# The opening of a convolution layer laid out anew: shifts as row products, the condition spread by TensorE, weight halves on GpSimd

## Chip, cores and metric

The kernel runs on one core of a Trainium2 chip. The metric is device time in microseconds. The kernel before takes 1960.24 us (median of three runs, 1960.0 to 1963.34).

## What is computed

One layer of a streaming encoder in fp32: 2048 tokens, width 1024, a short gated convolution, then a SwiGLU network. Both sub-layers are normalized before and after, and modulated by shift, scale and gate vectors that come from a condition vector c.

```python
def modulate(h, shift, scale):
    return h * (1.0 + scale[:, None, :]) + shift[:, None, :]

def short_conv_mixer(h, w_in, w_conv, w_out):
    gate_b, gate_c, v = jnp.split(h @ w_in, 3, axis=-1)
    u = gate_c * v
    conv = ...                       # causal, 3 taps, one filter for each channel
    return (gate_b * conv) @ w_out

c_act = jax.nn.silu(c)
mod = c_act @ ada_w[i] + ada_b[i]    # (1024) @ (1024 x 6144)
sh_m, sc_m, g_m, sh_f, sc_f, g_f = jnp.split(mod, 6, axis=-1)
h = modulate(rms_norm(x, norm_gains[i, 0]), sh_m, sc_m)
h = short_conv_mixer(h, ...)
x = x + g_m * rms_norm(h, norm_gains[i, 1])
h = modulate(rms_norm(x, norm_gains[i, 2]), sh_f, sc_f)
h = swiglu(h, ffn_w_gate_up[i], ffn_w_down[i])
return x + g_f * rms_norm(h, norm_gains[i, 3])
```

## The kernel before

**Products.** Tokens are handled in two passes (u = 0, 1) of 1024, each in two halves of 512. The phases follow one another: in0, out0, in1, out1, gu0, down0, gu1, down1 (input projection, output projection, gate and up, down). Each matrix product is split into 2 x 2 blocks and done with seven products instead of eight, P1 to P7. A product takes a sum of weight blocks and a feature: A11, A12, A22 (blocks of the normalized input) or sums of them, S1 to S4. In the first phase the four blocks of the input are called a (token half 0, channel half 0), b (0, 1), c (1, 0) and d (1, 1); e = a - c is the source of S3, d - e of S2, c + d of S1, b - S2 of S4.

Each operand is written as a high half, rounded to the fast matmul type (fp32r), and a low half, the rest. A product of one 128-row step k is three matmuls: high weight by high feature, low by high, high by low. High halves are copies by ScalarE (`high`, `upper`), low halves are subtractions by VectorE (`low`, `lower`, L458 to L465 for the weights). P5 of the first three groups is the exception: it multiplies whole fp32 words.

**Slots.** A slot is one product of one column group, four steps of three matmuls. In in0 the order is P1 of five groups (slots 0 to 4), P2 of five (5 to 9), then P7, P6, P5, P3 and P4 of the first three (10 to 24), and after that seven slots for each further group. The weights of a slot are prepared in stages, each some slots ahead of its use: `blocks` (load, SP's queue, 9 slots), `sums` (T3 and the P6 sum among them, 7), `high` (5), `low` (4). `advance(stage, slot)` takes a stage up to a slot. Work outside the slots is put off with `later`, `run` and `schedule`, all counted in slots. `sums_later("out", ...)` loads the blocks of the output projection, has GpSimd form the four sums of each group, and stores them to DRAM; it starts at slot 24 with two slots between steps. Every instruction is recorded through one helper, so each carries line L78, and each engine and each DMA queue runs its instructions in the order in which the program issues them.

**The opening** is `start()`, written out by hand (L1107 to L1387) up to slot 12. It does the following.

- SP loads the token rows of half 0 (xr), then for each quarter q of the channels the scale matrix (`load_scale`, laid out with one output on each partition) and the shift matrix (`load_shift`, laid out for a matmul), in turn with the blocks a to d and the weights. The rows of token half 1 are loaded before the last scale quarter.
- c comes on all 128 partitions by a DMA of ScalarE's queue (`c_half`, L144 to L146); ScalarE applies silu.
- `squares` (ScalarE), `factor` (VectorE, and GpSimd for the power -1/2), `diagonal` (VectorE) and `spread` (TensorE, copied out by ScalarE) give 1/rms along the free axis as `rb`.
- `scales` are row products on VectorE: one fused multiply and sum of 128 x 512 for each half row, 16 in all. `shifts` are eight fp32 matmuls for each quarter on TensorE (tile pms), with the row copied out by ScalarE and turned by two transposes (`turned`). `fold` puts both into mA (1 + scale, times the gain) and mB (shift).
- `mult` multiplies a feature by rb on VectorE, `shift` is a pass of ScalarE (times mA, plus mB) in place, `upper` and `lower` make the halves, `products` issues matmuls of chosen slots, `follow` takes the sums out of PSUM.
- `warm(n)` issues n fp32 matmuls of ones (tile wb), eight before the first factor and two before the first product.

Of the kernel before, what the change touches and what calls it, by code (L numbers as in the profile page):

```python
# [15 lines left out]
P = 128  # L16
# [15 lines left out]
EARLY = 5  # L32

# [16 lines left out]
def hybrid_conv_layer(  # L50
# [94 lines left out]
    for h in range(2):  # L145
        A.dma_start(c_half[h], c_row[:, h * CH : (h + 1) * CH].to_broadcast((P, CH)))  # L146
# [19 lines left out]
    def columns(row, r, n=4):  # L166

        A.copy(r[0:1, : n * P], row[0:1, : n * P])
        for c in range(n):
            PE.transpose(row[:, c : c + 1], r[0:1, c * P : (c + 1) * P], ident[0:1, 0:1])  # L170

    def mods_later(ms, pace):

        s2 = {(m, h): sb.tile([P, KD], F32, tag="ms", bufs=4, name=f"ms{m}_{h}") for m in ms for h in range(2)}
        for h in range(2):
# [6 lines left out]
            def load(i, half=half, todo=todo, tiles=tiles):  # L182
                if i < len(todo):
                    m, n = todo[i]
                    tiles[i] = raw(f"ada{m}_{half.start}_{n}")
                    SP.dma_start(tiles[i], ada[m - 1, n][:, half])
# [135 lines left out]
    class Blocks:  # L322
# [98 lines left out]
    class Weight:  # L421
# [685 lines left out]
    def start():  # L1107
        ph = phases[0]
        rb, mods, rows, xr = {}, {}, {}, {}
        f = Features(ph, from_xt(0), rb, 0)  # L1110
        s2 = [sb.tile([P, KD], F32, tag="ms", bufs=4, name=f"ms1_{h}") for h in range(2)]
        two = lambda ap: ap.rearrange("p (a b) -> p a b", a=2)
        pair_of = lambda t, i: t[:, 2 * i : 2 * i + 2, :]

# [6 lines left out]
        def load_scale(q):  # L1121

            t = mods[1, q] = big(f"ada1_{q}")
            for i in range(2):
                SP.dma_start(pair_of(t, i), two(ada[0, 2 * q + i]))

        def load_shift(q):

            t = mods[0, q] = big(f"ada0_{q}")
            for i in range(2):  # L1130
                SP.dma_start(pair_of(t, i), two(ada1[2 * q + i]))
# [10 lines left out]
        def factor(tok, meanwhile=lambda: None):  # L1142
# [4 lines left out]
            meanwhile()  # L1147
            return diagonal(at_once(steps), f"r{tok}")

        def shifts(q):  # L1150
            t = mods[0, q].rearrange("p a b -> p (a b)").rearrange("p (k n) -> p k n", k=KD)
            rows[q] = bank(f"pms{q}")
            for k in range(KD):
                PE.matmul(rows[q][0:1, :256], col(cact, k), t[:, k, :], start=k == 0, stop=k == KD - 1)

        def turned(q):
            columns(rows[q], mods[0, q][:, 0, :], 2)

        def scales(q, i):
# [4 lines left out]
        def fold(q):  # L1164
            n = slice(2 * q, 2 * q + 2)
            t = small(2, f"mf{q}")
            V.tensor_tensor(t, s2[0][:, n], s2[1][:, n], ALU.add)
            V.tensor_tensor(t, t, vt[:, VB + KD + n.start : VB + KD + n.stop], ALU.add)
            V.scalar_tensor_tensor(mA[0][:, n], t, 1.0, vt[:, VG + n.start : VG + n.stop], ALU.add, ALU.mult)
            V.tensor_tensor(mB[0][:, n], rows[q][:, :2], vt[:, VB + n.start : VB + n.stop], ALU.add)  # L1170

        def mult(key, k4):
            t = f.t[key][:, k4, :]
            V.tensor_tensor(t, t, rb[f.place[key][0]], ALU.mult)

        def shift(key, k4):
            t, k = f.t[key][:, k4, :], f.place[key][1] * 4 + k4
            A.activation(t, t, AF.Identity, bias=col(mB[0], k), scale=col(mA[0], k))

        def upper(op, k4):  # L1180
            if (op, 0) not in ph.A:
                ph.A[op, 0] = big(f"{ph.name}{op}h", F32R), big(f"{ph.name}{op}l", F32R)
            A.copy(ph.A[op, 0][0][:, k4, :], f.t[f.SOURCE[op]][:, k4, :])

        def lower(op, k4):
            hi, lo = ph.A[op, 0]
            V.tensor_tensor(lo[:, k4, :], f.t[f.SOURCE[op]][:, k4, :], hi[:, k4, :].bitcast(F32), ALU.subtract)
# [15 lines left out]
        load_scale(0)  # L1203
        load_shift(0)
        f.load("a")
        advance("blocks", 2)
        load_scale(1)
        load_shift(1)
        advance("blocks", 4)
        f.load("b")  # L1210
        load_scale(2)
        load_shift(2)
        advance("blocks", 7)
        load_shift(3)
        load_rows(1)
        load_scale(3)
# [5 lines left out]

        def split(key, op, ks):
            for k in ks:
                shift(key, k)
                upper(op, k)
                lower(op, k)
# [10 lines left out]
        warm(8)  # L1238


        squares(0, range(4))
# [12 lines left out]
        fold(0)  # L1254
        mult("a", 3)
        advance("low", 0)
        for k in range(2):
            shift("a", k)
            upper("A11", k)
            lower("A11", k)  # L1260
            advance("high", 1 + k)
            advance("low", 1 + k)
        products(0, range(2))
        scales(1, 0)
        scales(1, 1)
        shifts(1)
        advance("high", 4)
        advance("low", 4)
        products(3, range(2), range(1))
        turned(1)  # L1270
        fold(1)
        products(4, range(2), range(1))
        split("a", "A11", range(2, 4))
        products(0, range(2, 4))
        for k in range(4):
            mult("b", k)
        shifts(2)
        scales(2, 0)
        scales(2, 1)
        products(3, range(2, 4), range(1))  # L1280
        squares(1, range(2))
        turned(2)
        advance("high", 7)
        products(4, range(2, 4), range(1))
        advance("low", 7)
        squares(1, range(2, 4))
        fold(2)
        shifts(3)
        v = small(4, "v1")
        V.tensor_scalar(v, sq[1], EPS, None, ALU.add)  # L1290
        steps = root(v, "r1")
        next(steps)
        shift("b", 0)
        upper("A12", 0)
        scales(3, 0)
        lower("A12", 0)
        shift("b", 1)
        upper("A12", 1)
        scales(3, 1)
        dg = at_once(steps)  # L1300
        lower("A12", 1)
        turned(3)
        fold(3)
        dg = diagonal(dg, "r1")
        products(5, range(2), range(1))
        rb[1] = spread(dg, "r1")
        products(6, range(2), range(1))
        advance("sums", 12)
        shift("b", 2)
        upper("A12", 2)  # L1310
        mult("c", 0)
        lower("A12", 2)
        mult("c", 1)
        shift("b", 3)
        upper("A12", 3)
        lower("A12", 3)
        follow(0, range(3))
        mult("c", 2)
        mult("c", 3)
        products(5, range(2, 4), range(2))  # L1320
        follow(3, range(2))
        advance("high", 9)
        follow(5, range(1))
        advance("low", 8)
        follow(6, range(1))
        products(7, range(4), range(1))
        for k in range(4):
            shift("c", k)
        advance("low", 9)
        products(8, range(4), range(1))  # L1330
        follow(7, range(1))
        products(9, range(4), range(1))

# [3 lines left out]
        def e(k):  # L1337
            V.tensor_tensor(f.t["e"][:, k, :], f.t["a"][:, k, :], f.t["c"][:, k, :], ALU.subtract)
# [3 lines left out]
        advance("high", 10)  # L1342
        e(1)
        follow(8, range(1))
        advance("low", 10)
        lower("S3", 0)
        advance("high", 11)
        advance("low", 11)
        follow(9, range(1))
        lower("S3", 1)  # L1350
        e(2)
        advance("high", 12)
        e(3)
        advance("low", 12)
# [6 lines left out]

        for k in range(4):
            mult("d", k)
            shift("d", k)
        advance("sums", 15)
        advance("high", 15)
        for k in range(4):
            V.tensor_tensor(f.t["a"][:, k, :], f.t["d"][:, k, :], f.t["e"][:, k, :], ALU.subtract)
            upper("S2", k)
            if k:  # L1370
                advance("low", 12 + k)
# [6 lines left out]
        for k in range(4):  # L1378
            V.tensor_tensor(f.t["c"][:, k, :], f.t["c"][:, k, :], f.t["d"][:, k, :], ALU.add)
# [3 lines left out]
        f.s4()  # L1383
        for i, step in ((15, partial(f.high, "S4")), (16, partial(f.low, "S4")),
                        (17, partial(f.high, "A22")), (18, partial(f.low, "A22")),
# [30 lines left out]
    schedule(24, lambda: run(sums_later("out", range(4), 2)))  # L1416
# [98 lines left out]
```

## Time and profile before

| | |
|---|---|
| median of the runs | 1960.24 us (1960.0, 1960.24, 1963.34) |
| the profiled execution | 1961.33 us, span 1959.5 us |
| instructions | 24903 |
| TensorE (PE) busy | 1934.8 us, 8454 matmuls |
| VectorE (DVE) busy | 1446.5 us, 2069 |
| ScalarE (ACT) busy | 899.6 us, 1419 |
| GpSimd (POOL) busy | 343.8 us, 226 |
| moved by DMA | 462.14 MB, mean 236 GB/s |

Times in the profile count from the start of the span. A row of the timeline gives the start in us, the duration in us, engine, line, operation, output<-inputs with buffer numbers left out, sizes and a count where like instructions are merged, and in square brackets the idle time of the engine before it with what ended it. Weight tiles are named by phase and group with digits partly dropped: in4P<-in4b is a low half of a weight of group 4, in0b<-in0P an addition from PSUM. An engine's instructions that follow at once overlap a little, so that the distance from start to start is shorter than the duration.

### The profile page before, as it was taken

How to read it: one execution, taken by the hardware profiler on the slowest of the kernel's cores; microseconds unless marked ns; L12 is line 12 of the kernel's file. 1: busy time of each engine (PE TensorE's matmuls, PEld its weight loads, DVE VectorE, ACT ScalarE, POOL GpSimd, SP SyncE). 2: the span in 40 equal slices, each digit the busy share in tenths (PEclk: the TensorE clock that was granted, in tenths of full speed). 3: DMA queues.
4: the chain of work that ended last, by engine and by line, in shares of the span. 5: the costliest groups of instructions: out<-in, count | busy, mean ns of one | idle time of the engine just before them, and what ended most of it. 6: DMA issues, size and time to landing. Idle time of an engine off the chain costs nothing.

```text
span 1959.5 us, 24903 instructions
## 1 busy us (share of the span) xinstructions
PE 1934.8 (99%) x8454; PEld 1570.0 (80%) x8454; DVE 1446.5 (74%) x2069; ACT 899.6 (46%) x1419; POOL 343.8 (18%) x226
## 2 busy tenths in 40 slices
PE   8899999999999999999999999999999999999998
PEld 4678887878878888888888888888888888888886
DVE  4898898977998776997776755587776655665466
ACT  4543457634446743543333454473333333444452
POOL 0012112211221301243341410120100100111011
PEclk9999999999999999999999999999999999999999
DMA  9369979769996764777665977588654332386534
GB/s 390 138 227 373 339 253 349 268 225 371 323 324 216 279 232 149 238 241 244 213 214 183 313 281 269 192 287 279 203 192 140 127 137 97 118 321 226 196 134 133
DMA packets 207632, 462.14 MB, mean 236 GB/s; under 512 B 24465, under 2 KB 39953, under 8 KB 201105
## 3 DMA queue, kind: packets, MB, share of 16 engines
q1 hardware_dynamic: 181584, 406.40, 60.1%
q10 hardware_dynamic: 25920, 54.16, 7.3%
q8 instruction: 66, 1.08, 0.2%
q14 instruction: 62, 0.50, 0.1%
HBM read 329.38 MB, written 131.09 MB: 235 GB/s over the span
## 4 chain that ended last, share of the span: by engine, by line
PE 80%; DVE 8%; DMA 6%; ACT 3%; issue 2%; SPq 0%; ACTq 0%; POOL 0%; DVEq 0%
PE gu1P L78 21%; PE gu0P L78 18%; PE in0P L78 11%; PE down0P L78 11%; PE down1P L78 11%; PE in1P L78 3%; PE out1P L78 2%; PE out0P L78 2%; DMA x<-xx 1%; PE pms L78 1%; DMA kgu1P<-gu1P 1%; DVE in1b L78 0%; DVE in1y L78 0%; DVE gu0a L78 0%; DMA xr<-x_d 0%
## 5 line engine op out<-in xcount | busy, mean ns | idle before, releaser
L78 DVE TENSOR_TENSOR gu1a<-gu1P,gu1a 128x512 f32<-128x512 f32 x63 | 43.5, 691 | 108.5 <-PE gu1P L78 108.5
L78 DVE TENSOR_TENSOR gu0a<-gu0P,gu0a 128x512 f32<-128x512 f32 x63 | 43.3, 688 | 71.7 <-PE gu0P L78 68.8
L78 POOL TENSOR_TENSOR gu1a<-gu1a 128x512 f32<-128x512 f32 x11 | 19.0, 1731 | 360.0 <-DVE gu1g11s L78 39.9
L78 ACT COPY gu1a<-gu1P 128x512 f32<-128x512 f32 x42 | 24.7, 589 | 96.1 <-PE gu1P L78 85.0
L78 POOL TENSOR_TENSOR nq<-nq,nq 128x512 f32<-128x512 f32 x28 | 42.8, 1529 | 136.1 <-ACT nq L78 131.4
L78 ACT COPY gu0a<-gu0P 128x512 f32<-128x512 f32 x42 | 24.4, 586 | 82.2 <-PE gu0P L78 81.0
L78 DVE CUSTOM_DVE_ANT_0 ada<-ada,c 128x512 f32<-128x512 f32 x80 | 60.1, 762 | 0.0
L78 ACT COPY gu1g<-gu1P 128x512 f32<-128x512 f32 x24 | 14.1, 588 | 92.8 <-PE gu1P L78 88.0
L78 POOL TENSOR_TENSOR gu0a<-gu0a 128x512 f32<-128x512 f32 x11 | 19.4, 1767 | 170.6 <-ACT gu0a L78 45.3
L78 ACT COPY gu0g<-gu0P 128x512 f32<-128x512 f32 x24 | 14.1, 589 | 74.4 <-PE gu0P L78 71.0
L78 POOL TENSOR_TENSOR down0q<-down0q,down0q 128x512 f32<-128x512 f32 x14 | 21.0, 1502 | 148.1 <-ACT down0q L78 148.1
L78 ACT ACTIVATE nq<-xx 128x512 f32<-128x512 f32 x32 | 37.1, 1159 | 17.0 <-DVE xx L78 17.0
L78 POOL TENSOR_TENSOR down1q<-down1q,down1q 128x512 f32<-128x512 f32 x10 | 16.1, 1612 | 148.6 <-ACT down1q L78 148.5
L78 DVE TENSOR_TENSOR gu1g<-gu1P,gu1g 128x512 f32<-128x512 f32 x24 | 16.6, 691 | 24.4 <-ACT gu1g L78 23.0
L78 DVE TENSOR_TENSOR down2P<-down2P,down2P 128x512 fp32r<-128x512 f32 x14 | 11.2, 801 | 29.0 <-ACT down2P L78 29.0
L78 ACT ACTIVATE gu1a<-gu1a 128x512 f32<-128x512 f32 x42 | 26.6, 633 | 13.1 <-DVE xo L78 6.0
L78 ACT ACTIVATE gu0a<-gu0a 128x512 f32<-128x512 f32 x42 | 26.6, 634 | 7.3 <-DVE gu0a L78 6.1
L78 POOL TENSOR_TENSOR out1q<-out1q,out1q 128x512 f32<-128x512 f32 x14 | 19.9, 1422 | 55.2 <-ACT out1q L78 55.1
L78 POOL TENSOR_TENSOR out0q<-out0q,out0q 128x512 f32<-128x512 f32 x14 | 20.8, 1485 | 46.9 <-ACT out0q L78 29.7
L78 DVE TENSOR_TENSOR gu0g<-gu0P,gu0g 128x512 f32<-128x512 f32 x24 | 16.5, 689 | 14.3 <-ACT gu0g L78 12.9
L78 DVE TENSOR_TENSOR xx<-xx,zz 128x512 f32<-128x512 f32 x32 | 25.1, 784 | 1.1
L78 ACT ACTIVATE down0q<-down0z 128x512 f32<-128x512 f32 x16 | 18.4, 1153 | 14.9 <-DVE down0z L78 14.8
(3139 smaller groups left out, 6715.8 us busy)
## 6 DMA issues: line engine op xcount, KB each, us to landing
ada<-ada_d SPq DMA_DIRECT2D x64, 256.0 KB, 5.3
act0A<-gu0a SPq DMA_DIRECT2D x33, 256.0 KB, 3.5
act1A<-gu1a SPq DMA_DIRECT2D x33, 256.0 KB, 2.6
ada<-ada_d SPq DMA_DIRECT2D x16, 512.0 KB, 9.5
zz<-z SPq DMA_DIRECT2D x32, 256.0 KB, 5.7
xx<-xt_d SPq DMA_DIRECT2D x32, 256.0 KB, 5.5
x<-xx ACTq DMA_DIRECT2D x32, 256.0 KB, 5.4
down0S<-act0S SPq DMA_DIRECT2D x8, 1024.0 KB, 7.3
```

What stands on the lines that cost most here:

```text
L78: return tc.keep_in_program_order(f(*args, **kwargs))
```

## The change

- **Condition.** Only one partition receives c by DMA. Two fp32 matmuls with a row of ones spread it to 128 partitions in PSUM, and ScalarE applies silu from there.
- **Shifts.** Quarters 0 and 3 stay matmuls (`columns`, `turned`). Quarters 1 and 2 use the layout of the scales: of each quarter one row block is two fused row products of VectorE (`dots`), the other two multiplications of GpSimd (`dots_mult`) and one sum of ScalarE (`dots_sum`).
- **No shift pass.** `mult` becomes one VectorE instruction (times mA, times rb). The shift is a bias in `upper` for A11, A12 and A22, and a scalar in `lower` (a three-operand instruction); in e = a - c it cancels, and in the S2, S1 and S4 sources it is a scalar of a three-operand instruction.
- **GpSimd.** It takes the low halves of the weights of slots 4 to 7 and 10 to 39, and T3 and the P6 sum of the first three groups (six instructions).
- **Order.** Loads, warm matmuls (2, then 13 after the spreading, then 2) and steps of the opening stand in a new order. The rows of token half 1 come after all four quarters. The columns of quarter 0 stand before the spreading of r0.
- **Output sums** start at slot 42 instead of 24, with 1.25 slots between steps instead of 2.

The diff, cut:

```diff
+OUT_SUMS = 42
+LOW_ON_POOL = (4, 5, 6, 7) + tuple(range(10, 40))
+T3_ON_POOL = range(3)
...
-        A.dma_start(c_half[h], c_row[:, h * CH : (h + 1) * CH].to_broadcast((P, CH)))
+        A.dma_start(c_half[h][0:1, :], c_row[:, h * CH : (h + 1) * CH])
...
         def sum(self, op):
+            E = G if self.kind == "in" and self.grp in T3_ON_POOL else V
             if op in ("P7", "P6") and "T3" not in self.summed:
-                V.tensor_tensor(b["12"], b["22"], b["12"], ALU.subtract)
+                E.tensor_tensor(b["12"], b["22"], b["12"], ALU.subtract)
             if op == "P6":
-                V.tensor_tensor(b["11+"], b["12"], b["11+"], ALU.add)
+                E.tensor_tensor(b["11+"], b["12"], b["11+"], ALU.add)
...
-                V.tensor_tensor(w[:, 1, :n].bitcast(F32R), self.t, w[:, 0, :n], ALU.subtract)
+                (G if self.place in LOW_ON_POOL else V).tensor_tensor(w[:, 1, :n].bitcast(F32R), self.t, w[:, 0, :n], ALU.subtract)
...
+        def dots(m, q, i):
             for h in range(2):
-                t = mods[1, q][:, 2 * i + h, :]
-                V.tensor_tensor_reduce(t, t, c_half[h], 1.0, 0.0, ALU.mult, ALU.add, col(s2[h], 2 * q + i))
+                t = mods[m, q][:, 2 * i + h, :]
+                V.tensor_tensor_reduce(t, t, c_half[h], 1.0, 0.0, ALU.mult, ALU.add, col(s2[m, h], 2 * q + i))
+        def dots_mult(m, q, i):
+            for h in range(2):
+                t = mods[m, q][:, 2 * i + h, :]
+                G.tensor_tensor(t, t, c_half[h], ALU.mult)
+        def dots_sum(m, q, i):
+            t = pair_of(mods[m, q], i)
+            A.activation(t, t, AF.Copy, accum_out=col(s2[m, 0], 2 * q + i))
+            V.memset(col(s2[m, 1], 2 * q + i), 0.0)
...
-        def mult(key, k4):
-            V.tensor_tensor(t, t, rb[f.place[key][0]], ALU.mult)
-        def shift(key, k4):
-            A.activation(t, t, AF.Identity, bias=col(mB[0], k), scale=col(mA[0], k))
+        def mult(key, ks):
+            f.scale(key, ks)
+        def upper(op, k):
+            if op in ("A11", "A12", "A22"):
+                A.activation(planes(op)[0][:, k, :], f.t[key][:, k, :], AF.Identity, bias=shift_of(key, k))
...
+        def lower(op, k, E=V):
+            if op in ("A11", "A12", "A22"):
+                V.scalar_tensor_tensor(lo[:, k, :], f.t[key][:, k, :], shift_of(key, k), hi[:, k, :].bitcast(F32), ALU.add, ALU.subtract)
...
-        warm(8)
+        warm(2)
+        cb = [bank(f"cb{h}") for h in range(2)]
         for h in range(2):
-            A.activation(c_half[h], c_half[h], AF.Silu)
-        dg = factor(0)
+            PE.matmul(cb[h], one[0:1, :], c_half[h][0:1, :], start=True, stop=True)
+        warm(13)
+        squares(0, (0, 1))
+        for h in range(2):
+            A.activation(c_half[h], cb[h], AF.Silu)
+        squares(0, (2, 3))
+        steps = factor(0)
+        dots(1, 0, 0)
+        columns(0)
+        dg = diagonal(at_once(steps), "r0")
         rb[0] = spread(dg, "r0")
-        scales(0, 0)
-        scales(0, 1)
-        shifts(0)
-        advance("high", 0)
-        for k in range(3):
-            mult("a", k)
+        dots(1, 0, 1)
+        fold(1, 0)
         turned(0)
         warm(2)
+        mult("a", (0,))
+        fold(0, 0)
+        advance("high", 0)
+        upper("A11", 0)
...
-    schedule(24, lambda: run(sums_later("out", range(4), 2)))
+    schedule(OUT_SUMS, lambda: run(sums_later("out", range(4), 1.25)))
```

From there the new order in `start()`, with v for VectorE, g for GpSimd and s for ScalarE: A11 steps 0 and 1; row products of scale quarter 1 (v) and half of shift quarter 1 (g), weight low 4 (g); products of slots 0 to 2 and 3, 4 on steps 0 and 1; the rest of quarter 1 and A11 steps 2 and 3; products of slots 0 to 4 on them; quarter 2 in the same way; A12 steps 0 and 1; weight lows 5 and 6 (g); columns of shift quarter 3; products of slots 5 and 6; scale quarter 3, weight low 7 (g); the squares of token half 1; A12 steps 2 and 3; products; the factor of half 1; T3 of three groups (g); slots 7 to 9 with weight lows 10 to 12 and the P6 sums (g) beside them; e and S3 with the scaling of c; weight lows 13 to 15 (g); d and S2.

More of the change, by code (lines that the diff above doesn't have):

```diff
@@ L163, in col @@
         return t[:, k : k + 1]
[L166 to L170, printed above, removed]
     def mods_later(ms, pace):
@@ L1256, in start @@
         advance("low", 0)
[L1257 to L1262, printed above, removed]
+        mult("a", (1,))
+        lower("A11", 0)
+        upper("A11", 1)
+        advance("high", 2)
+        advance("low", 2)
+        lower("A11", 1)
         products(0, range(2))
-        scales(1, 0)
-        scales(1, 1)
-        shifts(1)
+        dots(1, 1, 0)
+        dots(1, 1, 1)
@@ L1267, in start @@
+        dots_mult(0, 1, 0)
         advance("high", 4)
         advance("low", 4)
[L1269 to L1280, printed above, removed]
-        squares(1, range(2))
-        turned(2)
-        advance("high", 7)
@@ L1284, in start @@
[L1284 to L1309, printed above, removed]
+        products(3, range(2), range(2))
+        fold(1, 1)
+        dots(0, 1, 1)
+        mult("a", (2,))
+        dots_sum(0, 1, 0)
+        fold(0, 1)
+        upper("A11", 2)
+        mult("a", (3,))
+        lower("A11", 2)
+        upper("A11", 3)
+        lower("A11", 3)
+        products(0, range(2, 4), range(5))
@@ new lines, in start @@
+        dots_mult(0, 2, 0)
+        dots(0, 2, 1)
+        dots_sum(0, 2, 0)
+        dots(1, 2, 0)
+        dots(1, 2, 1)
+        fold(1, 2)
+        mult("b", (0,))
+        fold(0, 2)
+        upper("A12", 0)
+        mult("b", (1,))
+        lower("A12", 0)
+        upper("A12", 1)
+        lower("A12", 1)
+        advance("high", 6)
+        advance("low", 6)
+        columns(3)
+        products(5, range(2), range(2))
+        turned(3)
+        dots(1, 3, 0)
+        dots(1, 3, 1)
+        fold(1, 3)
```

186 lines of the change are left out of this document (103 added, 83 removed).

## Prediction

> **What bounds the kernel now.** I read the page first, then busy time by stretches of 20 us, then the chain that ended last, then the timeline engine by engine from 0 to 190 us. The columns of the stretches are busy us of PE, PEld, DVE, ACT and POOL, then granted clock, DMA share and GB/s.
>
> ```profile
> PE 1934.8 (99%) x8454; PEld 1570.0 (80%) x8454; DVE 1446.5 (74%) x2069; ACT 899.6 (46%) x1419; POOL 343.8 (18%) x226
> ...
> 20.00:40.00 20.00, 18.65 (x72) 10.41 (x71) 11.86 (x31) 8.54 (x14) 0.00 (x0) 1.00 1.03 417
> 40.00:60.00 20.00, 18.72 (x78) 10.01 (x77) 16.12 (x44) 14.40 (x26) 1.38 (x1) 1.00 0.95 382
> 60.00:80.00 20.00, 17.98 (x71) 14.20 (x70) 17.33 (x29) 12.77 (x23) 0.00 (x0) 0.91 0.31 119
> 80.00:100.00 20.00, 18.31 (x61) 10.65 (x59) 18.09 (x24) 10.40 (x16) 0.00 (x0) 1.00 0.11 32
> ...
> 140.00:160.00 20.00, 20.00 (x90) 16.57 (x89) 19.79 (x27) 7.13 (x12) 8.43 (x5) 1.00 1.02 368
> ```
>
> PE is busy 99% of the span, so a gain must come from time in which PE does not multiply features. That time lies in the opening. GpSimd is idle there, and VectorE fills up: 11.9, 16.1, 17.3, 18.1 of 20 us, then 19.8.
>
> ```profile
> 127.05 139.02 PE in0P L78 x612
> ...
> 22.94 0.73 PE L78 MATMUL in0P<-in0A11h,in0P 128*128 128x512 f32 x2
> ...
> 84.20 1.29 DVE L78 TENSOR_TENSOR in0S2l<-in0a,in0S2h 128x512 fp32r<-128x512 f32 x2
> 84.94 0.19 PEld L78 LDWEIGHTS in0P<-in0S2l,in0P 128*128 128x128 f32 x1 [1.28 <-DVE in0S2l L78]
> ```
>
> From the chain, one product matmul costs 139.02/612 = 0.227 us. The first product starts at 22.94, and the last stage that PE has to wait for is the S2 feature: its fourth low half is written by VectorE at 84.20 + 0.60 + 0.69 = 85.5. After that PE multiplies nearly without a gap. I therefore cost the change by one question: when does VectorE write that S2 low half? Up to 85.5 PE owes only 13 slots of 12 matmuls, 156 x 0.227 = 35.4 us, so it is fed, not full.
>
> **The change, part by part: PE's front.** The order on PE becomes 2 warm matmuls, 2 that spread the condition, 13 warm, the shift columns of quarter 0, the spread of r0, the transposes, 2 warm, products.
>
> ```profile
> 1.64 10.16 PE L78 MATMUL wb<-w,one 128*128 128x512 f32 x16 [1.64 <-DVE w L78]
> ...
> 6.07 0.34 PEld L78 LDWEIGHTS wb<-w,one 128*128 128x128 f32 x1 [0.52 <-issue]
> 6.92 0.34 PEld L78 LDWEIGHTS wb<-w,one 128*128 128x128 f32 x1 [0.52 <-issue]
> ...
> 8.20 0.19 PEld L78 LDWEIGHTS wb<-w,one 128*128 128x128 f32 x1 [0.24 <-issue]
> 8.63 0.19 PEld L78 LDWEIGHTS wb<-w,one 128*128 128x128 f32 x1 [0.24 <-issue]
> ...
> 28.88 3.62 PE L78 MATMUL pms<-ada,cact 128*1 128x256 f32 x16
> 53.74 1.10 PE L78 MATMUL r1b<-r1d,one 128*128 128x512 f32 x2 [0.19 <-DVE r1d L78]
> 54.87 0.59 ACT L78 COPY r1r<-r1b 128x512 f32<-128x512 f32 x1 [3.24 <-PE r1b L78]
> 18.20 1.90 DVE L78 TENSOR_TENSOR in0a<-in0a,r0r 128x512 f32<-128x512 f32 x3 [1.72 <-DMA in0a<-xt_d]
> ```
>
> A warm matmul is two passes (8 gave 16), 0.85 us apart while cold, 0.43 after about 7.8. The first eight passes (2 warm, 2 spreading) end near 8.4; 13 x 2 x 0.43 = 11.2 brings 19.6; columns 3.6, spread 1.1, copy 0.6: the factor is in SBUF at 24.95, where before the scaling of feature a began at 18.20. VectorE's diagonal, its other row products and a fold end near 15.4 (three steps of 0.2 after 4 x 0.61 and 0.88, from 11.5 on); its next instruction waits for the factor, so it has nothing for some 9 us. First product: transposes and 2 warm more, about 27.3 (22.94 before).
>
> The condition's row must land before PE's third matmul, about 5.1.
>
> ```profile
> ident<-eye_d ACTq DMA_DIRECT2D x1, 64.0 KB, 8.7
> vt<-vec_d ACTq DMA_DIRECT2D x1, 56.0 KB, 4.1
> ```
>
> Issued at about 1.2, it lands between 5.3 and 9.9 by these two; I take 5.3, since vt is the nearest in size and place. The other end moves all that follows by up to 4.5 us.
>
> **What VectorE issues from 24.95 on.** The terms:
>
> ```profile
> 26.03 0.68 DVE L78 CUSTOM_DVE_ANT_0 ada<-ada,c 128x512 f32<-128x512 f32 x1
> 26.64 0.08 DVE L78 DVE_READ_ACCUMULATOR2_ANT ms<- 128x1 f32 x1
> 26.64 0.69 DVE L78 CUSTOM_DVE_ANT_0 ada<-ada,c 128x512 f32<-128x512 f32 x1
> ...
> 29.68 0.16 DVE L78 TENSOR_TENSOR mf<-ms,ms 128x2 f32<-128x2 f32 x1
> 29.87 0.16 DVE L78 TENSOR_TENSOR mf<-mf,vt 128x2 f32<-128x2 f32 x1
> ...
> 112.61 1.53 DVE L78 SCALAR_TENSOR_TENSOR in0y<-in0c,vt,in0y 128x512 f32<-128x512 f32 x2
> 13.15 0.88 DVE L78 TENSOR_SCALAR r0d<-ident,r0q 128x128 f32<-128x128 f32 x4 [1.14 <-POOL r0q L78]
> ```
>
> From start to start: a row product 0.61, a fold step 0.2, a two-input instruction 0.60 (1.29 less the last one's 0.69), one with a scalar besides 0.73 (an estimate: half of 1.53 is 0.77 with the last one's tail), a diagonal 0.88. Counted in program order: to A11's second low half 4.9 (two scalings, three weight lows, two lows, a fold step); to its fourth 8.15 (6 row products, a weight low, 5 fold steps, 2 scalings, 2 lows); to A12's second 7.55 (6, 5, 2, 2); to its fourth 6.15 (4, 4, 2, 2); then 13.2 (2 weight lows, diagonal, 5 additions from PSUM, 4 scalings of c, 4 e, 4 S3 lows, small ones); then d: 4 x (0.73 + 0.73 + 0.60) = 8.2. Sum 48.15.
>
> **What GpSimd does meanwhile, and what that costs VectorE.**
>
> ```profile
> 105.05 1.30 POOL L78 TENSOR_TENSOR out0b<-out0b,out0b 128x512 f32<-128x512 f32 x1 [55.02 <-DMA out0b<-w_out_d]
> 105.08 0.68 DVE L78 TENSOR_TENSOR in0b<-in0P,in0b 128x512 f32<-128x512 f32 x1
> 105.68 1.22 DVE L78 TENSOR_TENSOR in1P<-in1b,in1P 128x512 fp32r<-128x512 f32 x1
> ...
> 138.47 3.48 DVE L78 SCALAR_TENSOR_TENSOR in0y<-in0c,vt,in0y 128x512 f32<-128x512 f32 x2
> 139.67 3.43 POOL L78 TENSOR_TENSOR out0b<-out0b,out0b 128x512 f32<-128x512 f32 x2
> ```
>
> GpSimd's subtraction runs from 105.05 to 106.35. VectorE's addition with a PSUM input beside it keeps its 0.68; the weight low with two SBUF inputs takes 1.22 and ends 0.55 after GpSimd does. At 138 both queues are full, and two VectorE instructions take 3.48 while two of GpSimd's take 3.43: they take turns, and each GpSimd instruction holds VectorE for about 1.1. A weight low moved over thus saves 0.60 and costs up to 1.1. [...]
>
> Between 24.95 and S2, GpSimd gets weight low 4, two row products of quarter 2, lows 5 to 7, three T3, lows 10 to 12, three P6 sums, lows 13 to 15: 18 instructions, 19.8 us (quarter 1's two run free in VectorE's gap). Four of the five additions from PSUM run beside them: 2.4 back. With 0.5 of waiting for ScalarE, S2's last low half comes at 24.95 + 48.15 + 19.8 - 2.4 + 0.5 = 91.0, against 85.5: **5.5 us later**. No row shows GpSimd writing fp32r; I take the f32 price (same data), with 1.72 (half of 3.43) above and 0 below as ends.
>
> **What is saved, and why it buys nothing.** PE loses two column passes, 2 x 3.62; ScalarE loses 16 shift passes; the condition's copy to 128 partitions, 0.5 MB, leaves the DMA engines. PE waits for VectorE anyway (I get some 4 us of idleness before slot 3's low and 4 before A12's third block), and the first loads are ahead of the factor. If VectorE stops being the bound, these return. On SP's queue the rows of token half 1 move behind 1 MB more and land about 1 us later, still ahead of ScalarE's squares. ScalarE takes two row sums in time that the shifts leave.
>
> **Slots 19 to 39.** 21 lows go to GpSimd (21 x 0.5 = 10.5 us dearer to VectorE), while the out sums, 8 instructions there before, start at slot 42 (8.8 cheaper), and PSUM additions overlap.
>
> ```profile
> 141.87 1.77 DVE L78 TENSOR_TENSOR in4P<-in4b,in4P 128x512 fp32r<-128x512 f32 x1
> ...
> 146.22 0.62 PE L78 MATMUL in0P<-in0S4h,in4P 128*128 128x512 f32 x2
> ```
>
> The slack there is 146.22 - 143.6 = 2.6 us, so little may go wrong; I add 1 us. ScalarE's queue, which stores kept weights, now waits for GpSimd's lows; two slots of lag (5.4 us) cover about three of them.
>
> **Sum.** 5.5 + 1 = 6.5. The profiled execution took 1961.33 (span 1959.5), 1.1 above the median of 1960.24. On the median: **1966.7 us**.
>
> **The clock.** After ScalarE's late weight at 71.49 PE ran slowly:
>
> ```profile
> 71.49 0.51 PE L78 MATMUL in0P<-in0S3h,in2P 128*128 128x512 f32 x1 [1.79 <-ACT in2P L78]
> ...
> 72.92 1.06 PE L78 MATMUL in0P<-in0S3h,in0P 128*128 128x512 f32 x2
> ```
>
> Two matmuls took 1.06 instead of 0.45. The longer waits I expect before S2 may cost the same, 0 to 2 us; that goes into the range. [...]
>
> **Rivals.** (1) *GpSimd's work falls where VectorE waits anyway.* Its queue is empty before 22 us and VectorE has small gaps behind ScalarE. With none of the 18 held against VectorE, S2 comes at 73.6, 12 us earlier than before; the sign turns where (85.5 - 73.6)/1.1 = 11 of the 18 hold it. With five or six, -6: 1954 us. Against it: VectorE is busy 17.3 and 18.1 of 20 us from 60 on even before, and all the lower halves stand in a row behind one another. Chance 0.30. (2) *The two sides cancel*: the factor arrives earlier than 24.95 or VectorE's order leaves fewer waits, and S2 lands within 3.9 us of 85.5; 1956.3 to 1964.2 us. Chance 0.18. (3) *The steady part gives way too*: GpSimd's lows miss the 2.6 us of slack, or the denser out sums press on the DMA engines, whose share is 1.02 at 140 to 160; 4 to 10 us more, 1973. Chance 0.10. My own case, 1964.2 to 1971, holds 0.42.
>
> A change of under 0.2% (3.9 us) is about what can't be told from none. Faster 0.30, same 0.18, slower 0.52. Range 1950 to 1975: below it the better half of rival 1, above it the worse half of rival 3 and a late condition row.
>
> **What would show it.** First product near 27; VectorE idle from about 15 to 25; two-input instructions of VectorE lasting 1.2 to 1.8 beside POOL between 50 and 90; PE waiting for A12's third block and for S2 lows; S2's last low half near 91. Wrong if VectorE's means stay at 0.7, or if S2's comes before 82.

## The result, and the profile after

The changed kernel takes 1987.88 us (median; 1984.8 to 1989.66) against 1961.22 beside it on the same chip: 1.0133 times as long, 95% interval 1.0116 to 1.0151. That is 26.7 us slower, where 6.5 were forecast and 1975 was the upper end of the range. The profiled execution took 1989.16 (span 1987.4), near the top of its runs.

The page's busy times of the kernel after, then four stretches of 20 us (columns as before: PE, PEld, DVE, ACT, POOL, then granted clock, DMA share, GB/s):

```profile
PE 1946.5 (98%) x8436; PEld 1578.5 (79%) x8436; DVE 1460.8 (74%) x2045; ACT 888.6 (45%) x1408; POOL 416.4 (21%) x273
```

```profile
60.00:80.00 20.00, 16.12 (x56) 11.33 (x56) 18.04 (x22) 8.97 (x17) 14.82 (x10) 0.90 0.32 118
80.00:100.00 20.00, 15.86 (x58) 12.10 (x59) 19.53 (x24) 7.03 (x13) 6.01 (x5) 0.85 0.00 1
140.00:160.00 20.00, 15.71 (x62) 12.90 (x63) 19.72 (x23) 5.60 (x11) 12.38 (x9) 0.83 0.83 308
280.00:300.00 20.00, 15.04 (x53) 11.54 (x52) 18.07 (x34) 8.68 (x16) 2.59 (x2) 0.83 0.76 257
```

VectorE has 24 instructions fewer (2045 against 2069), yet it is busy for longer (1460.8 us against 1446.5). From 60 to 80 us it ran 22 instructions in 18.0 us, where 29 took 17.3 before. PE is short in three separate places: in the opening, with 1.9 and 2.5 us less than before in the two stretches up to 100, and then 4.3 and 5.0 us less at 140 to 160 and 280 to 300, where it had been busy all 20 us.

The timeline after, at the steps of the prediction and at PE's two late stalls:

```profile
30.31 1.03 PE L82 MATMUL in0P<-in0A11h,in0P 128*128 128x512 f32 x2
...
94.58 1.46 DVE L82 TENSOR_TENSOR in0S2l<-in0a,in0S2h 128x512 fp32r<-128x512 f32 x2
96.43 0.63 PE L82 MATMUL in0P<-in0S2h,in1P 128*128 128x512 f32 x2
...
144.29 1.22 PE L82 MATMUL in0P<-in0S4h,in3P 128*128 128x512 f32 x2 [6.28 <-ACT in0c L82]
...
285.30 1.22 PE L82 MATMUL in0P<-in0S4h,in10P 128*128 128x512 f32 x2 [4.96 <-ACT in0C L82]
```

The first product starts at 30.3 (22.94 before), S2's last low half ends at 96.0 (85.5 before), and PE then waits 6.3 us at slot 28 and 5.0 us shortly before out0.

The same matmul can be found in every trace, so the lateness of each kernel against the kernel before is read place by place. Each number below is the start of that matmul in the profiled execution less its start before (85.97, 140.78, 263.18 us); medians and ratios are of several runs each. Two runs of over 8000 us, one of the halves of slots 19 to 39 alone and one of the kernel before, are left out of them, and why they were so slow is not known.

| kernel | slot 14 (S2, in1P) | past slot 28 (A11, in5P) | before out0 (S2, in11P) | median us | ratio to before, interval |
|---|---|---|---|---|---|
| the change | +10.5 | +18.8 | +27.4 | 1987.88 | 1.0133 [1.0116, 1.0151] |
| halves back on VectorE | +6.6 | +7.5 | +15.7 | 1976.26 | 1.0081 [1.0066, 1.0096] |
| sums back at slot 24 | +10.7 | +19.8 | +19.8 | 1977.5 | 1.0085 [1.0067, 1.0104] |
| new opening alone | +6.0 | +7.1 | +7.1 | 1967.28 | 1.0037 [1.0024, 1.005] |
| new opening and its own halves | +7.1 | +11.2 | +11.2 | 1971.61 | 1.0057 [1.0042, 1.0073] |
| halves and T3 alone | +9.0 | +14.6 | +14.6 | 1973.83 | 1.0067 [1.0047, 1.0087] |
| halves of slots 19 to 39 alone | 0.0 | +5.5 | +5.5 | 1966.77 | 1.003 [1.0019, 1.0042] |
| idle subtractions | +9.2 | +16.5 | +16.5 | 1975.65 | 1.0075 [1.006, 1.009] |
| idle one-operand work | +1.5 | +3.2 | +3.2 | 1963.62 | 1.0018 [1.0009, 1.0028] |
| out sums at 42, pace 1.25, alone | +0.2 | +0.2 | +7.7 | 1967.45 | 1.0036 [1.0023, 1.0048] |
| out sums at 24, pace 1.25, alone | -0.4 | +0.5 | +0.5 | 1960.23 | 0.9992 [0.9983, 1.0001] |
| opening mended | +10.9 | +14.8 | +14.8 | 1973.17 | 1.0065 [1.005, 1.008] |
| opening mended again | -1.0 | +2.2 | +2.2 | 1964.29 | 1.0018 [1.0009, 1.0028] |

Three parts of the change are slower each by itself: the new opening 6.6 us, the halves and T3 13.0, the out sums 6.8 (each median less that of the kernel before beside it), together 26.4 of 26.7. That the total fits so well is partly luck, since the parts act on one another: the new opening with the sums (halves back) is 15.5 us slower where its two parts give 13.4, and the new opening with the halves (sums back) 16.7 where they give 19.6.

The first column also holds something that no edit was meant to change. ScalarE's copy of the first factor (r0r) ended at 28.4 us in the change and at 24.0 with the halves back, because TensorE began at half speed for a longer or a shorter time: the weight loads of its first matmuls are 0.85 us apart until 14.3 us in the change and 0.43 from 14.8 on, and 0.43 from 6.0 us on with the halves back (the section on why the prediction was wrong has rows). These 4.4 us are enough for all of the 3.9 between the two kernels at slot 14. The run times of the change spread over 4.9 us, and the same thing may be why; with one profile of each kernel that is not shown.

### The profile page after: what moved, and what is told of

Same layout as the page of the kernel before. It is cut to its first block, busy times and chain, and to the rows that moved or that the text cites. A ratio compares the mean times of both kernels' runs of the same rounds, so it can differ in the third digit from the quotient of the medians.

```text
span 1987.4 us, 24916 instructions
## 1 busy us (share of the span) xinstructions
PE 1946.5 (98%) x8436; PEld 1578.5 (79%) x8436; DVE 1460.8 (74%) x2045; ACT 888.6 (45%) x1408; POOL 416.4 (21%) x273
## 4 chain that ended last, share of the span: by engine, by line
PE 77%; DVE 8%; DMA 5%; issue 2%; ACT 2%; SPq 0%; ACTq 0%; POOL 0%; DVEq 0%; POOLq 0%
PE gu1P L82 21%; PE gu0P L82 20%; PE down0P L82 11%; PE down1P L82 10%; PE in0P L82 4%; PE out1P L82 4%; PE in1P L82 4%; PE out0P L82 2%; DMA in9b<-w_in_d 1%; DMA kgu2P<-gu2P 1%; DVE in1y L82 1%; DVE in1c L82 1%; DVE ada L82 0%; DMA gu1b<-w_gu_d 0%; DVE in1b L82 0%
## 5 line engine op out<-in xcount | busy, mean ns | idle before, releaser
L82 POOL TENSOR_TENSOR gu1a<-gu1a 128x512 f32<-128x512 f32 x11 | 18.8, 1707 | 359.5 <-DVE gu1g11s L82 39.5
L82 DVE CUSTOM_DVE_ANT_0 ada<-ada,c 128x512 f32<-128x512 f32 x84 | 66.9, 808 | 0.0
L82 ACT ACTIVATE nq<-xx 128x512 f32<-128x512 f32 x32 | 36.9, 1159 | 15.7 <-DVE xx L82 15.7
L82 ACT ACTIVATE gu1a<-gu1a 128x512 f32<-128x512 f32 x42 | 26.6, 633 | 13.4 <-DVE xo L82 6.0
L82 DVE TENSOR_TENSOR gu0g<-gu0P,gu0g 128x512 f32<-128x512 f32 x24 | 16.5, 689 | 14.1 <-ACT gu0g L82 12.7
L82 ACT ACTIVATE down0q<-down0z 128x512 f32<-128x512 f32 x16 | 18.4, 1150 | 14.9 <-DVE down0z L82 14.8
```

Of the source, the lines that this page charges most:

```text
L82: return tc.keep_in_program_order(f(*args, **kwargs))
```

## Experiments: taking the change apart

**Halves back on VectorE.** The changed kernel with

```diff
-LOW_ON_POOL = (4, 5, 6, 7) + tuple(range(10, 40))
-T3_ON_POOL = range(3)
+LOW_ON_POOL = ()
+T3_ON_POOL = ()
```

> The new opening with all 34 weight halves and the three additions of T3 back on VectorE; nothing else changed. Theory T (GpSimd's subtractions and VectorE's instructions take turns; this lengthens VectorE in the opening and again at slots 28 and 74): the stalls of 6.3 us before slot 28 and of 5.0 us before out0 go, so about 16 of the 27.9 us lost come back, and part of the opening's 10.5 as well: 1963 to 1972, VectorE's two-input instructions at 0.7 us again. Rival L (the new order of the opening and its first product at 30.3 us are the whole cost): 1983 to 1988. Rival O (the later and denser out sums): 1980 to 1988.

11.6 us came back, not 16 and more: the stall at slot 28 went, that before out0 stayed at 5.0 us. Theory T alone was too little: the time lies 4 us above its range, and what the rest is, the next runs say.

**Sums back.** The changed kernel with the schedule of the out sums as it was:

```diff
-    schedule(OUT_SUMS, lambda: run(sums_later("out", range(4), 1.25)))
+    schedule(24, lambda: run(sums_later("out", range(4), 2)))
```

> The changed kernel with the out sums put back to slot 24 and a pace of 2. Theory T: the stall before slot 28 stays or grows (the sums' fetches and VectorE work come on top), that before out0 shrinks by part: 1982 to 1990. Rival O: the 8 to 9 us that were lost between slots 66 and 77 come back, 1977 to 1980. Rival L: within 2 us of 1988.

10.4 us came back and the step before out0 vanished: rival O was right here. The lateness past slot 28 grew only from 18.8 to 19.8, so moving the sums away had relieved that place by about 1 us. Theory T's range of 1982 to 1990 was missed.

**Halves alone**: the kernel before with `LOW_ON_POOL`, `T3_ON_POOL` and the three lines of the diff that use them.

> The kernel before with the 34 halves and the T3 additions on GpSimd, and nothing else of the change. Theory T: slower by what the halves cost in the steady part and by some of the opening: 1970 to 1980. Rival L: no cost without the new order, 1959 to 1963. Rival O: 1961 to 1964, since the out sums stay at slot 24.

**New opening alone**: the changed kernel with both edits above.

> The new opening alone: the halves and T3 on VectorE and the out sums back at slot 24 with a pace of 2. If the three parts add up as the offsets of the traces say (7.5 us by slot 14 for the opening, nothing at slot 28, nothing before out0): 1967 to 1970. If the opening alone is free (rival H: its cost was the halves'): 1959 to 1963. If the parts hide one another: 1972 or more.

They are 13.0 and 6.6 us slower. The first lies in theory T's range, so rival L, by which the halves cost nothing without the new order, has fallen; the second lies in the range of parts that add up.

## Experiments: why the halves cost

**Idle subtractions.** In the kernel before, VectorE keeps its halves, and GpSimd is given work that nobody waits for, beside the same halves:

```diff
                 V.tensor_tensor(w[:, 1, :n].bitcast(F32R), self.t, w[:, 0, :n], ALU.subtract)
+                if self.place in IDLE_AT:
+                    for _ in range(4):
+                        G.tensor_tensor(spare, one, ident, ALU.subtract)
```

> The kernel before, its halves on VectorE as they were; where the change moves a half to GpSimd, GpSimd also runs four subtractions of 128x128 of two constant tiles into a tile that nobody reads, so nobody waits for them. Theory T (the two engines exclude one another while both read two operands of the scratchpad): VectorE's instructions beside them take longer than 0.69 us, in whole steps of GpSimd's own duration, and the time is 1965 to 1975. Rival D (the halves cost because GpSimd delivers them later): VectorE stays at 0.69 and the time at 1959 to 1963.

Four subtractions of 128x128 stand for each half: with tiles of a half's own size, 128x512, one pool of tiles wanted 25.2 KB per partition of SBUF where 19.7 were left. The kernel is 15 us slower, though nobody waits for their results. VectorE's groups from 60 to 100 us (count, then busy us and mean ns), in the kernel before:

```profile
L78 DVE TENSOR_TENSOR in0a<-in0d,in0e 128x512 f32<-128x512 f32 x4 | 2.7, 689 | 0.0
L78 DVE TENSOR_TENSOR in0S2l<-in0a,in0S2h 128x512 fp32r<-128x512 f32 x4 | 2.7, 689 | 1.2 <-ACT in0S2h L78 1.2
```

with the idle subtractions:

```profile
L80 DVE TENSOR_TENSOR in0a<-in0d,in0e 128x512 f32<-128x512 f32 x4 | 3.7, 936 | 0.0
L80 DVE TENSOR_TENSOR in0S2l<-in0a,in0S2h 128x512 fp32r<-128x512 f32 x4 | 3.7, 935 | 0.0
```

and one instruction beside them that reads PSUM, from the timeline of the same kernel:

```profile
65.75 0.68 DVE L80 TENSOR_TENSOR in0C<-in0P,in0C 128x512 f32<-128x512 f32 x1
```

VectorE's instructions with two SBUF operands lost 0.25 us each, and there about one of them ran to one GpSimd subtraction; the PSUM addition lost nothing (0.68, and a mean of 0.69 in the kernel before). Four times 0.25 is the 1.0 to 1.1 us that a 128x512 half costs. Rival D has fallen. Theory T is borne out in its main point but not in its form: the loss is not a whole step of GpSimd's own duration (0.25 us beside instructions of 0.788), and the time is 0.65 us above its range.

**Idle one-operand work**: the same places, with

```diff
-                        G.tensor_tensor(spare, one, ident, ALU.subtract)
+                        G.tensor_scalar(spare, one, 1.0, None, ALU.mult)
```

> The idle work on GpSimd again (136 instructions of 128x128 at the places of the moved halves, nobody waits for them), but each reads one operand: a tile of ones times 1.0. If only instructions of two operands exclude VectorE's: VectorE's pairs stay at 0.69 us and the time at 1959 to 1963. If GpSimd excludes VectorE's two-operand instructions whatever it reads itself: 1968 to 1977, as with two operands (1975.65), less where the instructions are shorter.

```profile
L80 DVE TENSOR_TENSOR in0a<-in0d,in0e 128x512 f32<-128x512 f32 x4 | 3.0, 771 | 0.0
L80 DVE TENSOR_TENSOR in0S2l<-in0a,in0S2h 128x512 fp32r<-128x512 f32 x4 | 3.0, 770 | 0.0
```

The groups as above: 0.08 us lost instead of 0.25, and 2.9 us in the time. Neither reading holds as written: one operand is not exempt, but costs a third. GpSimd's instruction itself shows a mean of 0.670 us against 0.788 with two operands, so VectorE is not held for the duration that the profile shows, but for a part of it: 0.25 of 0.788 us and 0.08 of 0.670. What sets that part is not shown.

**Halves of slots 19 to 39 alone**, in the kernel before: `LOW_ON_POOL = tuple(range(19, 40))`, T3 on VectorE.

> The kernel before with only the halves of slots 19 to 39 on GpSimd; the opening is untouched. If the 2.6 us by which a half's slot is ahead of its use took up what the exclusion costs, as the prediction had it: 1960 to 1963. If these halves cost by themselves (theory T, the stall before slot 28 seen with all halves): 1965 to 1968, and the first PE wait at 120 to 140 us. If that stall needs a late opening (rival H): 1960 to 1962.

6.1 us, with the opening untouched (+0.0 at slot 14). The rows of slot 28 in the changed kernel show how. VectorE, then GpSimd, then ScalarE:

```profile
135.21 2.56 DVE L82 SCALAR_TENSOR_TENSOR in0y<-in0C,vt,in0y 128x512 f32<-128x512 f32 x2
141.01 2.09 DVE L82 TENSOR_TENSOR in4b<-in4b,in4b 128x512 f32<-128x512 f32 x2
```

```profile
133.25 3.18 POOL L82 TENSOR_TENSOR in4P<-in4b,in4P 128x512 fp32r<-128x512 f32 x1 [0.25 <-ACT in4P L82]
140.50 1.26 POOL L82 TENSOR_TENSOR in3P<-in3b,in3P 128x512 fp32r<-128x512 f32 x1 [4.06 <-issue]
```

```profile
143.13 0.62 ACT L82 CAST in4P<-in4b 128x512 fp32r<-128x512 f32 x1 [2.77 <-DVE in4b L82]
143.66 0.58 ACT L82 COPY in0c<-in0P 128x512 f32<-128x512 f32 x1
```

The same place in the kernel before, VectorE's timeline and two stretches of 10 us:

```profile
124.36 1.41 DVE L78 TENSOR_TENSOR in4b<-in4b,in4b 128x512 f32<-128x512 f32 x2
125.69 1.53 DVE L78 SCALAR_TENSOR_TENSOR in0y<-in0c,vt,in0y 128x512 f32<-128x512 f32 x2
```

```profile
110.00:120.00 10.00, 10.00 (x46) 8.29 (x45) 9.86 (x17) 5.32 (x7) 0.00 (x0) 1.00 0.39 158
120.00:130.00 10.00, 9.32 (x42) 7.40 (x41) 9.86 (x18) 4.04 (x7) 0.00 (x0) 1.00 0.70 221
```

PE at 144.29 waits for a bank that ScalarE's copy in0c empties at 143.66. That copy stands in ScalarE's queue behind the cast of in4P, the cast waits for VectorE's weight sums in4b, and these stand on VectorE behind pairs that take 2.56 instead of 1.53 because GpSimd's halves run beside them. VectorE had been busy 9.86 of 10 us here before, so what it loses there has no slack to go into and reaches PE; this last step is read from the rows, not tested by itself. PE's wait at this place was 0.68 us in the kernel before, 4.26 with these halves alone and 0.98 in the new opening alone.

**The new opening with its own halves.** The new opening alone, and on GpSimd only the halves of slots 4 to 7 and 10 to 15 and the six instructions of T3.

> The new opening with the out sums at slot 24, and of the moved work only what falls into the opening: the halves of slots 4 to 7 and 10 to 15 and the six instructions of T3 and the P6 sums on GpSimd; the halves of slots 16 to 39 stay on VectorE. Reading N (from the factor to S2's last half the changed kernel took 67.6 us and the new opening with all halves on VectorE 67.1: in the new order these sixteen instructions are neutral, since VectorE waits there for token 1's factor): S2's last half 66 to 69 us after the factor's copy, 1966 to 1970, as the new opening alone (1967.28). Reading T (they cost as much as in the old opening, 9 us by slot 14): 1974 to 1978. A first product that comes late because TensorE's clock stays low for longer moves either by up to 5 us and is taken out by counting from the factor.

It lies between the readings: 10.5 us slower than the kernel before, 3.9 more than the new opening alone. From the end of the factor's copy (23.59) to that of S2's last half (92.71) it takes 69.1 us, in the new opening alone 67.2. These 1.9 us come out of three larger numbers, worked out from the timelines: VectorE does 9.6 us less of its own work (sixteen instructions at 0.60), GpSimd's turns hold it 14.4 us longer, and it waits 2.8 us less. Another 3.0 us are lost between slot 14 and the place past slot 28 (the lateness grows by 4.1 there, in the new opening alone by 1.1), though no half of slots 19 to 39 was moved. So the loss at slot 28 does not belong to those halves alone. In the old opening the halves cost 9.0 us by slot 14, and why it is so much more there is not shown.

## Experiments: the out sums

**Out sums at 42 alone**: in the kernel before, `schedule(42, lambda: run(sums_later("out", range(4), 1.25)))`.

> The kernel before with the out sums moved to slot 42 and a pace of 1.25, and nothing else. Theory S (the sums' blocks hold the ring of single tiles while the dot products of the next modulation want it from slot 54 on, so that their tile of c stays taken and ScalarE's copy out of PSUM waits for it): the stall before out0 of 5.0 us and about 7.7 us in all come back here without the new opening: 1966 to 1970. Rival H: 1960 to 1963, the stall needs the late opening or GpSimd's halves.

**Out sums early and dense**: in the kernel before, slot 24 kept, the pace 1.25.

> The kernel before with the out sums from slot 24 as they were, but at a pace of 1.25, so that they end at slot 54, where the dot products of the next modulation begin. Theory S (the stall before out0 comes from sums and dot products wanting the ring of single tiles at the same time): 1959 to 1964, no stall between slots 66 and 77. Rival P (the pace is the cost, wherever it lies): 1966 to 1970, with the stall at slots 30 to 54 instead.

The first costs 6.8 us, all of it in the last slots before out0; the second costs nothing. So the place is the cost and the pace alone is not. What happens at that place, from the timeline of the kernel with the sums at 42 (GpSimd, VectorE, ScalarE twice, PE):

```profile
257.03 4.63 POOL L78 TENSOR_TENSOR out3b<-out3b,out3b 128x512 f32<-128x512 f32 x3 [1.90 <-DMA out3b<-w_out_d]
```

```profile
256.98 2.95 DVE L78 TENSOR_SCALAR r2d<-ident,r2q 128x128 f32<-128x128 f32 x4
```

```profile
254.87 0.64 ACT L78 ACTIVATE c<-c 128x512 f32<-128x512 f32 x1 [2.27 <-DMA c<-c_row_d]
...
265.06 0.58 ACT L78 COPY in0C<-in0P 128x512 f32<-128x512 f32 x1 [8.53 <-DVE ms L78]
```

```profile
265.69 1.22 PE L78 MATMUL in0P<-in0S4h,in10P 128*128 128x512 f32 x2 [4.83 <-ACT in0C L78]
```

The last group's blocks arrive late, three subtractions run in one go, VectorE's diagonal takes 2.95 instead of the 0.88 of its like, ScalarE waits 2.3 us for the next condition row, and its copy out of PSUM then waits 8.5 us for VectorE. Whether the ring of tiles, as theory S says, or only this pile-up on VectorE delays the copy was not told apart: both go when the sums end before the dot products begin.

## Experiments: the new opening

**Opening mended.** The new opening alone, with these edits among others (token 1's squares in two places, its factor before `columns(3)`):

```diff
-        warm(13)
+        warm(6)
...
-        columns(0)
         dg = diagonal(at_once(steps), "r0")
         rb[0] = spread(dg, "r0")
+        columns(0)
...
-        dots_mult(0, 2, 0)
+        dots(0, 2, 0)
...
         products(5, range(2, 4), range(2))
-        steps = factor(1)
+        rb[1] = spread(dg, "r1")
```

> The new opening alone, mended at three places: the factor of token 0 is spread before the matmuls for the shift's columns and after 8 instead of 15 warming matmuls; the four dot products that GpSimd multiplied and ScalarE summed are VectorE's; the squares and the factor of token 1 come some 8 us earlier on ScalarE, VectorE and TensorE, and the first e rows before the halves of the weights at slots 9 to 12. Halves, T3 and out sums as before the change. If what costs 7.5 us is the late factor of token 1 (r1's copy at 64.4 against 55 us) and the late first product: S2's last half before 86 us, 1956 to 1963. If the fused operations of the new opening cost VectorE more than they save: 1966 to 1970, as the new opening alone.

A miss: 1973.17 us, with S2's last half at 96.4. VectorE's, TensorE's, ScalarE's and again VectorE's rows:

```profile
54.85 0.87 DVE L82 TENSOR_SCALAR r1d<-ident,r1q 128x128 f32<-128x128 f32 x4
```

```profile
61.53 1.86 PE L82 MATMUL r1b<-r1d,one 128*128 128x512 f32 x2
```

```profile
63.43 0.59 ACT L82 COPY r1r<-r1b 128x512 f32<-128x512 f32 x1 [6.29 <-PE r1b L82]
```

```profile
65.05 0.69 DVE L82 TENSOR_TENSOR in3P<-in3b,in3P 128x512 fp32r<-128x512 f32 x1 [7.13 <-ACT in3P L82]
```

Token 1's diagonal was ready at 55.7, but its spread stood behind the matmuls of slots 5 and 6 and began at 61.5. ScalarE waited 6.3 us for it with the next weights' casts behind, and VectorE waited 7.1 us for those.

**Opening mended again.** The spread goes ahead of those matmuls, the squares after the first two A12 halves, and the weights of slots 12 to 14 are cast after the first e row:

```diff
+        rb[1] = spread(dg, "r1")
         products(5, range(2, 4), range(2))
-        rb[1] = spread(dg, "r1")
```

> As the first mended opening (token 0's factor spread before the columns, 8 warming matmuls, all dot products on VectorE), but token 1's factor no longer waits behind 24 matmuls of slots 5 and 6: its spread is issued ahead of them, its four squares come after the first two A12 halves on ScalarE instead of before, and the weights of slots 12 to 14 are cast right after the first e row. Theory F (the place of token 1's factor in the in-order queues is what cost the mended opening its 7 us of idle VectorE at 58 to 65 us): r1's copy at 52 to 56 us, S2's last half at 82 to 87, 1956 to 1963. Rival W (VectorE's own work in the new opening is the bound): S2's last half at 92 to 96, 1967 to 1973.

```profile
52.17 0.59 ACT L82 COPY r1r<-r1b 128x512 f32<-128x512 f32 x1 [2.55 <-PE r1b L82]
...
83.11 1.46 DVE L82 TENSOR_TENSOR in0S2l<-in0a,in0S2h 128x512 fp32r<-128x512 f32 x2
```

The copy comes at 52.2 and S2's last half ends at 84.6: theory F was right on the place, and the time is 1.3 us above its range. The mended opening is 1.0 us ahead of the kernel before at slot 14 and 2.2 behind past slot 28. That VectorE's three-operand forms (S4: 2.73 us here, 2.29 as one plain instruction of 128x2048 before) are what the full stretch then gives back is argued from such rows, not tested alone. The two mended openings differ in some other steps too, such as columns of quarter 3 and row products that changed places, so the 8.9 us between them are not those of the spread alone. No version run here is faster than the kernel before.

## Why the prediction was wrong, step by step

- **PE's front.** The order was right and VectorE waited for the factor as forecast (12.1 us, where about 9 were forecast). The first product came at 30.3 instead of 27.3, since TensorE ran at half speed until 14.6 us instead of 7.8. The front of the kernel after, and the same instructions in the kernel with the new opening alone:

```profile
5.35 3.78 PE L82 MATMUL cb<-c,one 1*128 1x512 f32 x4
9.05 14.10 PE L82 MATMUL wb<-w,one 128*128 128x512 f32 x26
```

```profile
5.07 1.98 PE L82 MATMUL cb<-c,one 1*128 1x512 f32 x4
6.98 11.43 PE L82 MATMUL wb<-w,one 128*128 128x512 f32 x26
```

  TensorE's weight loads in the kernel after show the end of the slow phase, between 0.34 and 0.19 us each:

```profile
13.48 0.34 PEld L82 LDWEIGHTS wb<-w,one 128*128 128x128 f32 x1 [0.52 <-issue]
...
14.83 0.19 PEld L82 LDWEIGHTS wb<-w,one 128*128 128x128 f32 x1 [0.24 <-issue]
```

  With this front the factor's copy ended at 28.4, 27.8, 24.0, 23.6 and 23.6 us in five kernels. The forecast of 24.95 lies between, but it took the length of the cold phase from one trace as fixed, and 3.4 us of the profiled lateness is this (28.38 against 24.95). The condition row landed at 5.3 as taken.
- **The opening's sum.** From the factor to S2's last half 66.05 us were forecast (91.0 - 24.95) and 67.7 measured (96.04 - 28.38). Size and make-up were both right within 2 us. Worked out from the timeline, VectorE's own work took 48.3 us (48.15 forecast), GpSimd's turns held it for 16.7 (the time of its instructions above that of their like without GpSimd; 17.4 forecast, the 19.8 less 2.4), and it waited 2.6 (0.5 forecast). S2 came 5.0 us later than forecast, 3.4 from the late factor and 1.6 from this sum. The terms fit the new order less well without the halves. With the sixteen instructions back on VectorE and quarter 2's two row products still on GpSimd they give 48.15 + 16 x 0.60 + 2 x 1.1 + 0.5 = 60.5, and that kernel took 67.5. Of the 7.0 missing, 4.6 are waits of VectorE (5.1 where I had allowed 0.5; the longest, 1.9 us, for casts behind token 1's factor), and 1.9 are turns: quarter 1's row products started on GpSimd only when the factor was there, instead of in VectorE's gap, and four VectorE instructions right behind it took 1.66 to 1.77 us instead of 0.7.
- **GpSimd's price.** About 1.1 us for each half, and nothing for the additions from PSUM (0.68 us beside GpSimd): shown by the idle subtractions. VectorE's kinds that suffer are more than I counted: the dot products (1.74 to 1.78, against 0.68 with GpSimd idle) and the diagonal (3.31 against 0.88), in the kernel after:

```profile
33.71 1.78 DVE L82 CUSTOM_DVE_ANT_0 ada<-ada,c 128x512 f32<-128x512 f32 x1
...
64.46 3.31 DVE L82 TENSOR_SCALAR r1d<-ident,r1q 128x128 f32<-128x128 f32 x4
```

- **Slots 19 to 39: the step that failed.** "The slack there is 146.22 - 143.6 = 2.6 us ... I add 1 us": these halves alone cost 6.1 us, and in the change the lateness grew by 8.3 between slot 14 and the place past slot 28. The slack was read at one weight half, at 142 us; the stage's limit lay 15 us earlier, on VectorE, which was 9.86 of 10 us busy. The 10.5 us "dearer to VectorE" stood in my own sum; most of it should have been charged. It is not a plain sum, though: with only the opening's halves on GpSimd the lateness grew by 4.1 us there too.
- **The out sums.** I booked their move as 8.8 us cheaper for VectorE and kept its cost in a rival. It relieved slot 28 by about 1 us and cost 6.8 us where they landed, beside the dot products. This is the second mis-sized term: I did not look at what already ran just before out0. Of the 20.9 us by which the profiled lateness before out0 (27.4) exceeds the forecast (6.5), 5.0 arose by slot 14, 7.3 at slot 28 and 8.6 before out0.
- **Rivals.** Rival 3 named both late places, with 4 to 10 us for them together; they took 8.3 and 8.6. Its mechanisms were not those seen: at slot 28 VectorE is held rather than the halves being late for their use, and the denser pace by itself cost nothing (1960.23). Rival 1, GpSimd's work falling into VectorE's waits, does not describe the change: its turns held VectorE for 16.7 us in the opening.
- **Savings.** That PE, ScalarE and DMA savings buy nothing held in the change. The opening mended again, which has an earlier factor among other moves, is at slot 14 11.5 us ahead of the change and 7.0 ahead of the new opening alone. The first mended opening has its first factor early too and is 10.9 us behind the kernel before at slot 14, so an earlier factor by itself is not shown to be worth anything.

## What to carry to other kernels

Before work goes from VectorE to GpSimd, look at VectorE's busy time in short stretches of the stage where it will run: if it is full, each two-operand instruction moved can cost VectorE more than it frees (up to 1.1 us against 0.60 here), and GpSimd work that nobody waits for cost as much (15.0 us, the halves and T3 13.0). Slack is read on the engine that sets the stage, not at the instruction that moves. When a chain of small steps over several engines is moved in in-order queues, list for each step what stands ahead of it: here one spread, four squares and three casts, placed elsewhere among other steps, moved the time by 8.9 us.

## What the runs showed of the hardware

- With equal first instructions, TensorE ran at half speed (weight loads 0.85 us apart, 0.43 after it) until about 5.0 us after the start with the new opening alone and until 14.6 in the change, and the first factor's copy ended between 23.6 and 28.4 us in five kernels.
- GpSimd's hold on VectorE went with GpSimd's elements and operands, and was shorter than its shown duration: 0.25 us of 0.788 for 128 columns with two operands, 0.08 of 0.670 with one, and 1.1 us of 1.50 for 512 columns with two (a dot product of 1.78 us instead of 0.68 beside a weight half). VectorE's instructions with one SBUF operand can suffer too: the diagonal of four 128x128 took 3.31 us instead of 0.88 beside GpSimd's T3.
